# MLA queries made with their features on partitions, in a one-core hybrid encoder block

## The chip, the cores and the metric

The kernel runs on one core of a Trainium2 chip. The metric is device time in microseconds (us) of one execution of the whole block; lower is better. Engines are named as in the profile: PE is the matrix engine (PEld its weight loads), DVE the vector engine, ACT the scalar engine, POOL the GpSimd engine, SP the engine whose queue issues most DMAs.

## The reference, cut to what matters

The block normalises x, multiplies by one input matrix, runs a Mamba-2 mixer (SSD) and a multi-head latent attention (MLA) side by side, projects both out, and then runs a memory cross-attention and a convolutional feed-forward. All is f32, with 512 tokens and width 1024. The change concerns the queries of MLA alone:

```python
q_lat, kv_lat, k_rope = jnp.split(u, [MLA_Q_RANK, MLA_Q_RANK + MLA_KV_RANK], axis=-1)   # 384, 256, 32
q = (rmsnorm(q_lat, q_norm_w) @ w_q_up).reshape(b, s, MLA_HEADS, MLA_NOPE + MLA_ROPE)   # 16 heads of 64 + 32
q_nope, q_rope = jnp.split(q, [MLA_NOPE], axis=-1)
q_rope = apply_rope(q_rope, cos, sin)        # halves t1, t2 of 16: t1*cos - t2*sin, t1*sin + t2*cos
sc = einsum(q_nope, k_nope) + einsum(q_rope, k_rope)
p = softmax(where(mask, sc * (MLA_NOPE + MLA_ROPE) ** -0.5, min))
o = einsum(p, v)
```

## The kernel before, in words

Every f32 product is made of three matmuls (`mm3`, lines 103 to 105): each operand is split into a high part in the matrix engine's f32 format and the rest (`split`, lines 94 and 95: a copy on ACT, then a subtraction on DVE), and the terms high x high, high x low and low x high are added in PSUM. Weights come as pages: `wload` (line 148) has SP load a raw page into one of three `wr` tiles, `wsplit` (lines 156 to 158) splits it into one of four `wh`/`wl` pairs, with half of the subtraction on POOL in the later stages. PSUM has three `acc` banks, two `tr`, two `s` and one `pv`.

The normalised latents lie in five tiles `LT` with features on partitions and all 512 tokens along the row; three of them (384 features) feed the queries. They are filled 128 tokens at a time by `lat_q` and `lat_kv` (through `lat_norm`, lines 614 to 623: a square on ACT, a power on POOL at line 142, a scaling on DVE at line 619, transposes on PE at line 119, splits).

Queries are made four heads at a time by `q_up`. For each of four token tiles, nine matmuls of 384 columns take LT as the stationary operand and the weight page as the moving one, so that tokens lie on partitions (lines 718 to 720). ACT copies the bank to `qrow` (721), and four POOL instructions rotate the rotary features (724 to 727). Later `prep` makes each head ready: `k_pair` makes the keys of two heads by six matmuls of 512 columns, then four PE transposes bring the head's 96 query features onto partitions, and a split writes them into `qts[h % 2]`. There are two query tiles and two key tiles, used by even and odd heads in turn.

The attention loop overlaps heads: `scores(i + 1)`, `prep(i + 2)`, `probs_T(i)` and `pv(i)`, with units of other work put in between (`fills`: the output projection's parts `out_part`, the memory keys and values). `q_up(0)` is named by the operation `U` near the end of the list of the last SSD group; the other three calls stand in the attention loop after heads 1, 5 and 9.

The program order is only a priority. A list scheduler with a timeline model places each engine's instructions when it thinks them ready, and the order it finds is fixed at build time; each engine, and each DMA queue, then runs its list in order and waits at whatever is not ready. Parts of the output projection store and reload their sums through DRAM on the SP queue (`x_d` stores at line 658, loads at line 652), the same queue that issues all weight loads.

Of the kernel before, what the change touches and what calls it, by code (L numbers as in the profile page):

```python
# [7 lines left out]
F32 = mybir.dt.float32  # L8
# [54 lines left out]
def tile_block(ctx, tc, x, mem, positions, norm_mix_w, w_in, ssd_conv_w, ssd_conv_b, ssd_dt_bias,  # L63
# [166 lines left out]
    dec = base.tile([P, 3, NT, SSD_H], F32, name="dec")  # L230
    cenT = base.tile([P, NT, SSD_H], F32, name="cenT")
    acT = dram.tile([NT, SSD_H, P], F32, name="acT")
    memT_d = dram.tile([P, 2, KD, NMEM], F32, name="memT_d")
# [179 lines left out]
    nc.vector.tensor_copy(cosb[:, :, H2:], cosb[:, :, 0:H2])  # L413
    nc.vector.tensor_scalar(sinb[:, :, 0:H2], sinb[:, :, H2:], -1.0, None, ALU.mult)


# [262 lines left out]

    qrow = [k4([P, 2, 4, QH], "qrow") for _ in range(2)]  # L680
    kts, qts = [], []
# [18 lines left out]
    st = {}  # L700
    rts = [k1([P, 4, ROPE], "rt") for _ in range(2)]
    wkh, wkl = (page(n).rearrange("p i (n c) -> p i n c", n=2) for n in ("wkh", "wkl"))
# [6 lines left out]

    def q_up(q4):  # L710
        wq = mla_w_q_up[0][:, q4 * 4 * QH:(q4 + 1) * 4 * QH].rearrange("(k p) c -> p k c", p=P)
        pa = wpage(wq[:, 0:2], 2, 4 * QH)
        pb = wpage(wq[:, 2:3], 1, 4 * QH)
        st["q"] = []
        for t in range(NT):
            acc = acc_bank()[:, 0:4 * QH]
            for k in range(3):
                hi, lo = (pa[0][:, k], pa[1][:, k]) if k < 2 else (pb[0][:, 0], pb[1][:, 0])
                mm3(acc, (LT[k][:, 0, tsl(t)], LT[k][:, 1, tsl(t)]), (hi, lo), k == 0, k == 2)
            r = qrow[t // 2][:, t % 2]  # L720
            nc.scalar.copy(r.rearrange("p h c -> p (h c)"), acc)
            tm = rts[t % 2]
            bc = lambda a: a.unsqueeze(1).broadcast_to([P, 4, a.shape[1]])
            nc.gpsimd.tensor_tensor(tm[:, :, 0:H2], r[:, :, NOPE + H2:], bc(sinb[:, t, 0:H2]), ALU.mult)
            nc.gpsimd.tensor_tensor(tm[:, :, H2:], r[:, :, NOPE:NOPE + H2], bc(sinb[:, t, H2:]), ALU.mult)
            nc.gpsimd.tensor_tensor(r[:, :, NOPE:], r[:, :, NOPE:], bc(cosb[:, t]), ALU.mult)
            nc.gpsimd.tensor_tensor(r[:, :, NOPE:], r[:, :, NOPE:], tm, ALU.add)
            st["q"].append(r)

# [30 lines left out]
    def prep(h):  # L760
        if h % 4 == 0:
            kv_page(h // 4)
        if h % 2 == 0:
            k_pair(h % 4 // 2)
        ps = acc_bank()
        for t in range(NT):
            transpose(ps[0:QH, tsl(t)], st["q"][t][:, h % 4])
        split(qts[h % 2][0:QH, 0], qts[h % 2][0:QH, 1], ps[0:QH])

# [65 lines left out]
    def do(op, i):  # L835
        g, c = seq[i]
        if op == "z":
            z_unit(g, zn.pop(0))
        elif op == "l":
            late.pop(0)()  # L840
        elif op == "d":
            ssd_d(*seq[i - 1])
        elif op == "a":
            ssd_a(*seq[i + 1])
        elif op == "b":
            ssd_b(g, c)
        elif op == "i":
            lat_init()
        elif op[0] == "q":
            lat_q(int(op[1]))  # L850
        elif op[0] == "k":
            lat_kv(int(op[1]))
        elif op[0] == "p":
            part(int(op[1]))
        elif op == "s":
            setup_kq1()
        elif op == "U":
            q_up(0)
        elif op == "S":
            setup_kq2()  # L860
# [38 lines left out]
    for i in range(-1, MLA_H):  # L899
# [12 lines left out]
        if i >= 0:  # L912
            pv(i)
        if i % 4 == 1 and i + 3 < MLA_H:
            q_up((i + 3) // 4)
    for u in fills:
# [280 lines left out]
```

## Time and profile before

| | |
|---|---|
| median of 3 runs | 993.86 us (993.31 to 996.02) |
| the profiled execution, its own time | 995.55 us |
| its span, first to last instruction | 993.8 us |
| busy over the span | PE 98%, DVE 67%, ACT 53%, POOL 28% |
| DMA moved | 114.12 MB, mean 115 GB/s |
| mean granted PE clock | 0.995 of full speed |

The span is what the trace covers; the rest of the profiled execution's time lies around it. Matmuls are pipelined, so the duration of one is longer than the time by which it moves the next one along; the distance between two starts tells what it takes of the engine.

### The profile page before, as it was taken

What the parts mean: (1) busy time and instruction counts of PE and PEld (TensorE: products, weight loads), DVE (VectorE), ACT (ScalarE), POOL (GpSimd) and SP (SyncE); (2) the same over time, 40 slices, a digit from 0 to 9 for tenths busy, and PEclk for the clock granted to TensorE, in tenths of its full rate; (3) what the DMA queues carried; (4) which work ended last, traced back from release to release, by engine and by line L of the source; (5) the groups of instructions that cost most, each with busy time, mean ns of one, the idle gap of its engine ahead of it and who ended that gap; (6) DMA issues with size and microseconds to landing.
All of it is one profiled execution on the core that took longest, in us unless ns stands there. A gap on an engine that the chain in (4) does not pass through costs nothing.

```text
span 993.8 us, 15965 instructions
## 1 busy us (share of the span) xinstructions
PE 972.2 (98%) x5865; PEld 869.5 (87%) x5865; DVE 661.6 (67%) x1226; ACT 524.4 (53%) x1078; POOL 281.2 (28%) x360
## 2 busy tenths in 40 slices
PE   7999999998999999999999999999999999999997
PEld 6889898897899999999988899888888888888886
DVE  5989999868779787763644444676666666622553
ACT  5677776655477777763434433444444444421442
POOL 2016547566653547452343313000000000000000
PEclk9999999999899999999999999999999999999999
DMA  7653432316423336242341212233323322332462
GB/s 232 193 184 101 118 107 76 98 48 186 145 78 102 118 121 216 85 160 83 98 127 64 65 64 86 74 97 107 105 85 96 112 89 85 107 127 88 150 224 90
DMA packets 96453, 114.12 MB, mean 115 GB/s; under 512 B 5799, under 2 KB 82407, under 8 KB 95992
## 3 DMA queue, kind: packets, MB, share of 16 engines
q1 hardware_dynamic: 94680, 106.78, 34.0%
q0 software_dynamic: 1696, 6.33, 2.2%
q8 instruction: 46, 0.75, 0.3%
q14 instruction: 31, 0.25, 0.1%
HBM read 104.67 MB, written 8.42 MB: 114 GB/s over the span
## 4 chain that ended last, share of the span: by engine, by line
PE 83%; DVE 7%; DMA 3%; ACT 3%; POOL 2%; issue 2%; SPq 0%; POOLq 0%; DVEq 0%; ACTq 0%
PE acc L103 22%; PE acc L105 22%; PE acc L104 22%; PE tr L119 3%; PE s L103 2%; PE s L105 2%; PE s L104 2%; PE pv L809 2%; DMA aE<-acT 2%; DVE wl L157 1%; ACT aE L542 1%; DMA x_d<-lat 1%; DMA wr<-in_w_in_dram 1%; PE acc L119 1%; DVE cu L432 1%
## 5 line engine op out<-in xcount | busy, mean ns | idle before, releaser
L103 PE MATMUL acc<-Ah,wh 128*128 128x512 f32 (+1 forms) x560 | 215.7, 385 | 0.2 <-ACT Ah L94 0.2
L104 PE MATMUL acc<-Al,wh 128*128 128x512 f32 (+1 forms) x560 | 215.4, 385 | 0.1
L105 PE MATMUL acc<-Ah,wl 128*128 128x512 f32 (+1 forms) x560 | 215.1, 384 | 0.0
L95 DVE TENSOR_TENSOR wl<-wr,wh 128x1024 fp32r<-128x1024 f32 (+1 forms) x99 | 119.9, 1213 | 102.1 <-ACT wh L94 100.6
L94 ACT CAST wh<-wr 128x1024 fp32r<-128x1024 f32 (+1 forms) x99 | 101.8, 1031 | 135.5 <-PE acc L104 65.3
L158 POOL TENSOR_TENSOR wl<-wr,wh 128x512 fp32r<-128x512 f32 (+2 forms) x64 | 105.1, 1651 | 103.6 <-ACT wh L156 98.2
L142 POOL TENSOR_TENSOR rs<-ms,neg_half 128x1 f32<-128x1 f32 x18 | 10.4, 580 | 404.4 <-DVE ms L140 393.5
L103 PEld LDWEIGHTS acc<-Ah,wh 128*128 128x128 f32 x560 | 105.2, 188 | 20.4 <-ACT Ah L94 0.5
L105 PEld LDWEIGHTS acc<-Ah,wl 128*128 128x128 f32 x560 | 105.3, 188 | 20.1
L104 PEld LDWEIGHTS acc<-Al,wh 128*128 128x128 f32 x560 | 105.3, 188 | 19.9 <-DVE Al L95 0.4
L103 PE MATMUL acc<-wh,Ah 128*128 128x256 f32 (+1 forms) x304 | 90.4, 298 | 1.7 <-ACT Ah L94 1.7
L105 PE MATMUL acc<-wh,Al 128*128 128x256 f32 (+1 forms) x304 | 89.1, 294 | 0.3 <-DVE Al L95 0.3
L104 PE MATMUL acc<-wl,Ah 128*128 128x256 f32 (+1 forms) x304 | 88.9, 294 | 0.0
L156 ACT CAST wh<-wr 128x1024 fp32r<-128x1024 f32 (+2 forms) x64 | 65.5, 1027 | 38.5 <-PE acc L105 12.8
L1091 DVE SCALAR_TENSOR_TENSOR cbuf<-acc,fcw,cbuf 128x511 f32<-128x511 f32 (+1 forms) x88 | 65.6, 747 | 26.6 <-ACT cbuf L1089 25.0
L157 DVE TENSOR_TENSOR wl<-wr,wh 128x512 fp32r<-128x512 f32 (+2 forms) x64 | 55.8, 873 | 40.2 <-ACT wh L156 40.0
L103 PEld LDWEIGHTS acc<-wh,Ah 128*128 128x128 f32 x304 | 58.9, 194 | 2.9 <-ACT Ah L94 2.1
L104 PEld LDWEIGHTS acc<-wl,Ah 128*128 128x128 f32 x304 | 58.9, 194 | 0.5
L105 PEld LDWEIGHTS acc<-wh,Al 128*128 128x128 f32 x304 | 58.6, 193 | 0.9 <-DVE Al L95 0.6
L793 POOL TENSOR_SCALAR p<-p,ri 128x128 f32<-128x128 f32 (+1 forms) x64 | 34.6, 543 | 68.8 <-DVE ri L792 68.0
L1089 ACT ACTIVATE cbuf<-acc,fcb,fcw 128x512 f32<-128x512 f32 x44 | 34.3, 779 | 24.0 <-PE acc L105 24.0
L104 PE MATMUL acc<-wl,act 128*128 128x512 f32 (+1 forms) x112 | 40.5, 363 | 0.0
(370 smaller groups left out, 2450.5 us busy)
## 6 DMA issues: line engine op xcount, KB each, us to landing
wr<-in_w_ffn_up_dram SPq DMA_DIRECT2D x44, 512.0 KB, 3.5
wr<-in_w_ffn_down_dram SPq DMA_DIRECT2D x33, 512.0 KB, 3.6
wr<-in_w_in_dram SPq DMA_DIRECT2D x26, 512.0 KB, 3.8
wr<-in_w_out_dram SPq DMA_DIRECT2D x16, 512.0 KB, 3.7
aE<-acT POOLq DMA_DIRECT2D x16, 256.0 KB, 3.5
wr<-in_w_mem_k_dram SPq DMA_DIRECT2D x8, 512.0 KB, 3.6
wr<-in_w_mem_v_dram SPq DMA_DIRECT2D x8, 512.0 KB, 3.9
wr<-in_w_mem_q_dram SPq DMA_DIRECT2D x8, 512.0 KB, 3.4
```

The source lines that it names most:

```text
L94: first = nc.scalar.copy(hi, src)
L95: nc.vector.tensor_tensor(lo, src, f32(hi), ALU.subtract)
L103: nc.tensor.matmul(acc, lhsT=lh, rhs=rh, start=first, stop=False)
L104: nc.tensor.matmul(acc, lhsT=lh, rhs=rl, start=False, stop=False)
L105: nc.tensor.matmul(acc, lhsT=ll, rhs=rh, start=False, stop=last)
L119: nc.tensor.transpose(dst, src, ident[:n, :n])
L156: nc.scalar.copy(hi, raw)
L157: nc.vector.tensor_tensor(lo[:, 0:a // 2], raw[:, 0:a // 2], f32(hi[:, 0:a // 2]), ALU.subtract)
L158: nc.gpsimd.tensor_tensor(lo[:, a // 2:], raw[:, a // 2:], f32(hi[:, a // 2:]), ALU.subtract)
L793: nc.gpsimd.tensor_scalar(p_, p_, ri, 1.0, ALU.mult, ALU.mult)
L1089: nc.scalar.activation(u, acc, AF.Identity, scale=fcw[:, 2, m:m + 1], bias=fcb[:, m:m + 1])
L1091: nc.vector.scalar_tensor_tensor(u[:, s:], acc[:, :T - s], fcw[:, 2 - s, m:m + 1], u[:, s:], ALU.mult, ALU.add)
```

## The change

Queries are made with features on partitions from the start. `q_rope(g)` makes the rotary features of eight heads at once: the first halves of all eight (8 x 16 = 128 rows) in one bank, the second halves in another, with the weights stationary and LT moving, 512 columns at a time. It rotates them there with cosine and sine tables that have features on partitions (`csT`, made once by eight copies on POOL, eight PE transposes and two ACT copies), and keeps them split in `rq`. `q_pair(pr)` makes the plain features of two heads in one bank, splits them into the two query tiles, and copies the rotary rows of both heads from `rq` by four DMAs. Nothing transposes queries any more. The weights are loaded by pieces: for the rotary features rows of 32 numbers per head, for the plain ones rows of 64. `q_rope(0)` stands where `q_up(0)` stood, `q_rope(1)` after head 4, and `q_pair` in `prep` of every even head. The scratch that POOL-issued DMAs use is set to 8192 bytes per partition.

```diff
+    csT = base.tile([P, 2, T], F32, name="csT")
...
+    csr = k4([P, 2, NT, 8, H2], "csr")
+    for i, tab in enumerate((cosb, sinb)):
+        for t in range(NT):
+            nc.gpsimd.tensor_copy(csr[:, i, t], tab[:, t, H2:].unsqueeze(1).broadcast_to([P, 8, H2]))
+        ps = tr_bank()
+        for t in range(NT):
+            transpose(ps[:, tsl(t)], csr[:, i, t].rearrange("p h c -> p (h c)"))
+        nc.scalar.copy(csT[:, i], ps)
...
-    qrow = [k4([P, 2, 4, QH], "qrow") for _ in range(2)]
+    rq = [k4([P, 2, T], "rq", F32R) for _ in range(2)]
-    rts = [k1([P, 4, ROPE], "rt") for _ in range(2)]
...
-    def q_up(q4):
...
+    def q_rope(g):
+        raw = base.tile([P, 3, 8, ROPE], F32, name="wr", tag="wr", bufs=3)
+        for k in range(3):
+            nc.sync.dma_start(raw[:, k], mla_w_q_up[0][tsl(k), :].rearrange("p (h c) -> p h c", h=MLA_H)[
+                :, 8 * g:8 * g + 8, NOPE:])
+        hi = base.tile([P, 3, 2, 8, H2], F32R, name="wh", tag="wh", bufs=4)
+        lo = base.tile([P, 3, 2, 8, H2], F32R, name="wl", tag="wl", bufs=4)
+        for k in range(3):
+            hv, lv = (a[:, k].rearrange("p s h c -> p h s c") for a in (hi, lo))
+            split(hv, lv, raw[:, k].rearrange("p h (s c) -> p h s c", s=2))
+        acc = []
+        for s in range(2):
+            acc.append(acc_bank())
             for k in range(3):
+                w = [a[:, k, s].rearrange("p h c -> p (h c)") for a in (hi, lo)]
+                mm3(acc[s], w, (LT[k][:, 0], LT[k][:, 1]), k == 0, k == 2)
+        for s in range(2):
+            a, b = f32(rq[s][:, 0]), f32(rq[s][:, 1])
+            nc.vector.tensor_tensor(b, acc[s], csT[:, 0], ALU.mult)
+            nc.vector.tensor_tensor(a, acc[1 - s], csT[:, 1], ALU.mult)
+            nc.gpsimd.tensor_tensor(b, b, a, ALU.add if s else ALU.subtract)
+            nc.scalar.copy(rq[s][:, 0], b)
+            nc.vector.tensor_tensor(rq[s][:, 1], b, f32(rq[s][:, 0]), ALU.subtract)
+
+    def q_pair(pr):
+        raw = base.tile([P, 3, 2, NOPE], F32, name="wr", tag="wr", bufs=3)
+        for k in range(3):
+            nc.sync.dma_start(raw[:, k], mla_w_q_up[0][tsl(k), :].rearrange("p (h c) -> p h c", h=MLA_H)[
+                :, 2 * pr:2 * pr + 2, 0:NOPE])
+        hi = base.tile([P, 3, P], F32R, name="wh", tag="wh", bufs=4)
+        lo = base.tile([P, 3, P], F32R, name="wl", tag="wl", bufs=4)
+        split(hi, lo, raw.rearrange("p k h c -> p k (h c)"))
+        acc = acc_bank()
+        for k in range(3):
+            mm3(acc, (hi[:, k], lo[:, k]), (LT[k][:, 0], LT[k][:, 1]), k == 0, k == 2)
+        for e in range(2):
+            q = qts[e]
+            split(q[0:NOPE, 0], q[0:NOPE, 1], acc[e * NOPE:(e + 1) * NOPE])
+            r = H2 * (2 * pr % 8 + e)
+            for s in range(2):
+                nc.sync.dma_start(f32(q[NOPE + H2 * s:NOPE + H2 * (s + 1)]), f32(rq[s][r:r + H2]))
...
         if h % 2 == 0:
             k_pair(h % 4 // 2)
-        ps = acc_bank()
-        for t in range(NT):
-            transpose(ps[0:QH, tsl(t)], st["q"][t][:, h % 4])
-        split(qts[h % 2][0:QH, 0], qts[h % 2][0:QH, 1], ps[0:QH])
+            q_pair(h // 2)
...
-            q_up(0)
+            q_rope(0)
...
-        if i % 4 == 1 and i + 3 < MLA_H:
-            q_up((i + 3) // 4)
+        if i == 4:
+            q_rope(1)
...
-    nc = _bacc.Bacc("TRN2", target_bir_lowering=False, num_devices=1)
+    nc = _bacc.Bacc("TRN2", target_bir_lowering=False, num_devices=1, dynamic_dma_scratch_size=8192)
```

## Rows read from the trace of the kernel before

**Rows 1.** The page: busy time by engine (PE alone), and the chain that ended last.
```profile
PE 972.2 (98%) x5865; PEld 869.5 (87%) x5865; DVE 661.6 (67%) x1226; ACT 524.4 (53%) x1078; POOL 281.2 (28%) x360
PE 83%; DVE 7%; DMA 3%; ACT 3%; POOL 2%; issue 2%; SPq 0%; POOLq 0%; DVEq 0%; ACTq 0%
```

**Rows 2.** Stretches: length; busy PE, PEld, DVE, ACT, POOL; clock, DMA share, GB/s.
```profile
40.00:100.00 60.00, 60.00 (x357) 52.66 (x356) 54.07 (x102) 43.58 (x87) 20.60 (x26) 1.00 0.46 140
250.00:268.00 18.00, 17.69 (x115) 17.07 (x116) 13.40 (x34) 10.14 (x24) 12.69 (x21) 0.83 0.46 138
268.00:440.00 172.00, 171.88 (x1259) 164.65 (x1259) 136.89 (x331) 126.50 (x323) 87.32 (x134) 1.00 0.39 127
```

**Rows 3.** Timeline of PE around a head's query transposes: start, duration, instruction, count.
```profile
325.94 0.60 PE L119 MATMUL acc<-cst,qrow 128*96 128x128 f32 x4
326.38 0.49 PE L119 MATMUL tr<-cst,p 128*128 128x128 f32 x3
...
330.13 0.34 PE L105 MATMUL acc<-wh,lt 128*128 128x384 f32 x1
...
332.05 0.33 PE L104 MATMUL acc<-wl,lt 128*128 128x384 f32 x1
...
339.68 0.40 PE L103 MATMUL acc<-lt,wkh 128*128 128x512 f32 x1
...
341.07 0.49 PE L119 MATMUL acc<-cst,qrow 128*96 128x128 f32 x3
```

**Rows 4.** Groups by line and shape, PE: busy time and mean ns of one.
```profile
L103 PE MATMUL acc<-wh,lt 128*128 128x384 f32 x48 | 17.2, 358 | 0.4 <-ACT lt L94 0.3
L119 PE MATMUL acc<-cst,qrow 128*96 128x128 f32 x64 | 10.1, 272 | 0.0
```

**Rows 5.** Busy time on tile `qrow` alone: length, PE, PEld, ACT, POOL, clock, DMA.
```profile
236.00:440.00 204.00, 10.09 (x64) 7.32 (x64) 7.67 (x16) 27.57 (x64) 0.98 0.41 131
```

**Rows 6.** Groups by line: two on DVE from 236 to 440 us, one on POOL.
```profile
L95 DVE TENSOR_TENSOR qt<-acc,qt 96x512 fp32r<-96x512 f32 x16 | 10.8, 674 | 0.3 <-ACT qt L94 0.3
L95 DVE TENSOR_TENSOR wl<-wr,wh 128x384 fp32r<-128x384 f32 x3 | 2.8, 935 | 0.4 <-ACT wh L94 0.2
...
L158 POOL TENSOR_TENSOR wl<-wr,wh 128x512 fp32r<-128x512 f32 (+2 forms) x64 | 105.1, 1651 | 103.6 <-ACT wh L156 98.2 <-issue 3.6 <-PE acc L105 1.6
```

**Rows 7.** Timeline of PE before the attention: the first query matmuls and a stall.
```profile
239.64 0.34 PE L103 MATMUL acc<-wh,lt 128*128 128x384 f32 x1
...
247.68 0.34 PE L104 MATMUL acc<-wl,lt 128*128 128x384 f32 x1
250.09 0.90 PE L119 MATMUL tr<-cst,qkl 128*128 128x128 f32 x3 [2.07 <-DVE lt L95]
```

**Rows 8.** Timelines of POOL and of DVE in the same stretch.
```profile
246.65 0.47 POOL L726 TENSOR_TENSOR qrow<-qrow,cosb 128x128 f32<-128x128 f32 x1
...
248.17 1.07 POOL L142 TENSOR_TENSOR rsl<-msl,neg_half 128x1 f32<-128x1 f32 x2
...
248.76 0.62 DVE L619 SCALAR_TENSOR_TENSOR qkl<-lat,rsl,qkl 128x384 f32<-128x384 f32 x1 [2.17 <-POOL rsl L142]
```

**Rows 9.** DMA queue, packets and share of 16 engines; issues by tile, KB each, us to landing.
```profile
q1 hardware_dynamic: 94680, 106.78, 34.0%
...
wr<-in_mla_w_q_up_dram SPq DMA_DIRECT2D x4, 384.0 KB, 4.5
...
x_d<-xs__689 SPq DMA_DIRECT2D x4, 128.0 KB, 1.7
...
x_d<-xs__692 SPq DMA_DIRECT2D x4, 128.0 KB, 3.8
```

**Rows 10.** SP: first query loads, one later load, a wait (us, times, longest).
```profile
206.01 18.01 SPq L148 DMA_DIRECT2D wr<-in_mla_w_q_up_dram  x2
...
349.87 0.38 SPq L148 DMA_DIRECT2D wr<-in_w_mem_k_dram  x1
...
SPq L658 <- DVE xs__689 L657: 10.7, 2, 9.1
```

More of the change, by code (lines that the diff above doesn't have):

```diff
@@ L708, in tile_block @@
     yt = base.tile([P, T], F32, name="yt", tag="L", bufs=5)
-    def q_up(q4):
[L711 to L714, printed above, removed]
-        for t in range(NT):
-            acc = acc_bank()[:, 0:4 * QH]
-            for k in range(3):
[L718 to L728, printed above, removed]
@@ L764, in prep @@
             k_pair(h % 4 // 2)
-        ps = acc_bank()
-        for t in range(NT):
-            transpose(ps[0:QH, tsl(t)], st["q"][t][:, h % 4])
-        split(qts[h % 2][0:QH, 0], qts[h % 2][0:QH, 1], ps[0:QH])
+            q_pair(h // 2)
     POFF = (384, None, 0, 512)
```

## The prediction

> **What bounds the kernel now.** I read the page first: PE is busy for 98% of the span and makes up 83% of the chain that ended last [rows 1]. The busy times by stretch then show where the queries live. From 268 to 440 us, the attention, PE is busy 171.88 of 172.00 us at full clock, with DVE at 80% and ACT at 74% [rows 2]: what PE no longer has to issue there comes off the time, unless something new makes it wait. Just ahead of that, from 250 to 268 us, the granted clock averages 0.83 [rows 2]. As the clock has two levels, 1.2 and 2.4 GHz, PE ran at the lower one for about a third of these 18 us, and (1 - 0.83) x 18 = 3.1 us were lost. The timeline shows what came before: from 239.64 to 247.68 us PE ran 26 of the first query matmuls among other work, then it stood idle for 2.07 us [rows 7]. The other timelines say why. DVE waited 2.17 us for the power on POOL that the last latent tile needs, and POOL had run rotations of the first queries just before it [rows 8].
>
> The price of a matmul is not its duration. A transpose lasts 272 ns [rows 4], but four of them move PE's next instruction by 326.38 - 325.94 = 0.44 us, so one costs 0.11. In the same way a 384-column matmul costs (332.05 - 330.13) / 11 = 0.1745 us and a 512-column one (341.07 - 339.68) / 6 = 0.232 us [rows 3].
>
> **The change, part by part.** *Transposes.* The 64 query transposes go [rows 4]: 64 x 0.11 = 7.0 us of PE. The tables need eight new ones early on: +0.9 us, since PE has no idle time from 40 to 100 us [rows 2].
>
> *Query matmuls.* Before there are 4 x 4 x 9 = 144 of 384 columns (one of their three lines shows 48, [rows 4]), after it 2 x 18 + 8 x 9 = 108 of 512 columns: 144 x 0.1745 = 25.1 us against 108 x 0.232 = 25.0 us. They move the same number of columns; -0.1 us.
>
> *ACT, DVE, POOL.* The 16 copies to `qrow` (7.7 us of ACT) and 64 rotations (27.6 us of POOL) go [rows 5]. ACT gets six 512-column copies instead; by the copies just named, of 384 columns at 0.48 us, that is about 4 us. DVE gets eight multiplications and four subtractions of 512 columns, by the query split at 0.674 us [rows 6] about 8 us, and the subtractions for the weight splits that POOL shared, eight times 0.935 us at most [rows 6]. Both lie in stretches where DVE has a fifth free; I take zero, and up to 2 us if they delay a bank. POOL gets four 512-column additions at 1.65 us [rows 6] and eight small copies. The eight copies have POOL's 39 idle us of 40 to 100 to lie in, while DVE, 90% busy there [rows 2], gets nothing. That the scratch for POOL's DMAs is set anew has no row; between no cost and one landing of 3.8 us [rows 9] I take none, as POOL issues nothing new.
>
> *Weight loads on SP.* Eight loads become 6 + 24 smaller ones, and 32 row copies are new: 54 more issues, at 0.38 us [rows 10] 20 us of a queue that otherwise mostly waits for buffers. A rotary group has 384 x 8 = 3072 rows of 128 bytes. The mean packet of this queue took 0.34 x 16 x 993.8 us / 94680 = 57 ns of one DMA engine [rows 9], whatever its size. So a group takes 3072 x 57 / 16 = 10.9 us and a pair's 768 rows 2.7 us; the row that is nearest, 4.5 us for 384 KB in longer rows [rows 9], is the lower end. The first query loads were out by 224.0 us [rows 10], 15.6 us ahead of their first matmul at 239.64 [rows 7], so even 10.9 us stay hidden. I take zero; the cover ends at 15.6 us.
>
> *Row copies.* The copies for the odd head of a pair wait for the scores of the head two before, and the queue behind them waits too: projection stores and reloads, and weight loads. A pair needs four issues (1.5 us) and a landing between 1.7 and 3.8 us [rows 9], 3.2 to 5.3 us. PE meanwhile has `k_pair` and `q_pair` (15 x 0.232 = 3.5 us), four transposes (0.44 us), `pv` and the fills. The copies may also stand behind a store that itself waits, 9.1 us at the longest [rows 10]. So a pair costs between 0 and 9.1 + 5.3 - 3.9 = 10.5 us. I take zero, because the keys' tiles were already rewritten under the same kind of wait and PE idled 0.12 us in the whole stretch [rows 2].
>
> *The first query pass.* `q_up` could start as soon as one token tile of latents was there; `q_rope` needs all four. The 26 matmuls before the stall (26 x 0.1745 = 4.5 us) must come after it. In their place the scheduler can pull projection parts forward, and POOL's power is no longer behind rotations. Between +4.5 us and more, and -2.1 (the stall) - 3.1 (the clock), I take zero.
>
> *Sum:* -7.0 + 0.9 - 0.1 = -6.2 us. The profiled execution took 995.55 us, 1.75 around its span and 1.7 above the median of 993.86; taken off the median that is 987.7, so **988 us**. The measurement can tell about 0.3%, 3 us, from no change.
>
> A rule of the skill speaks against this change. The Trainium skill, "DMA: Bandwidth & Descriptors" (Specifications and Rules for kernel authors), says that pieces below 512 bytes are read, modified and written, and that small transfers should be put together; by it the 128-byte rows would cost more than the mean packet, up to twice if each is moved twice; no row here shows the price of so short a row. That makes the fourth rival below, whose time is worked out from the rows alone.
>
> **The rivals.** *B, the stall goes with the rotations.* With POOL free of them the last latent tile comes earlier, and both the idle 2.1 us and the clock's 3.1 us vanish: 993.9 - 6.2 - 5.2 = 982.5 us. For it speaks POOL's order in the stretch, against it the loss of 26 matmuls as filling.
>
> *C, the first pass leaves a hole.* Nothing takes the place of the 26 matmuls: -6.2 + 4.5 = -1.7, and with another stretch at 1.2 GHz of the size seen up to +1.4; 993 us. For it: projection parts lean on loads and stores of the same SP queue. Against it: PE ran such parts right after the stall, from pages loaded before it.
>
> *D, the rotary rows come late.* Even and odd heads' query tiles are both rewritten by DMA between the scores of one head and the next. If PE waits at the first scores of each pair, the change loses from 6.2 / 8 = 0.8 us a pair. With one landing of 1.7 us uncovered per pair it is 993.9 - 6.2 + 8 x 1.7 = 1001 us. For it: the queue is strictly in order and full of stores that wait for DVE [rows 10]. Against it: the scheduler lets PE pull other ready matmuls forward, and the stretch had 0.12 us idle.
>
> *E, the short rows come late.* At twice the mean packet time a rotary group takes 21.9 us, 6.3 more than the lead: 994 us. For it there is only the rows' length; against it, the lead and DMA engines that are 39% busy [rows 2].
>
> **How the numbers follow.** The forecast has 0.46, B 0.15, C 0.19, D 0.16, E 0.04. The forecast's own span is 985 to 991. The range takes in B's upper part, C and E, and D where it costs little more than it gives: 982 to 997, which leaves out some 0.13 of D and 0.05 of B. Below 990.9 lie the forecast, B and the edge of C: faster 0.62. C's rest and E give within 0.3%: 0.21. D makes slower: 0.17.
>
> **What would show it.** Right: no `qrow` transposes, 108 query matmuls spaced 0.232 us, PE busy without waits from the first pass to the end of attention, and all of the gain found between 240 and 440 us. B: no idle and full clock around 250 us. C: a longer wait of PE for the latents' splits there, with a lower clock behind it. D: PE waiting for DMAs into the query tiles at the first scores of even heads. E: ACT's split of the rotary weights waiting for its load. The forecast is wrong if PE's idle time between 200 and 440 us grows by more than 3 us, or if the time changes outside that stretch by more than the 0.9 us of the new transposes.

## The result and the profile after

The changed kernel takes 1009.35 us (1008.58 to 1009.43, four runs) against 993.89 us (993.31 to 996.02) for the one before: a ratio of 1.015, 95% interval 1.0132 to 1.0167. It is slower by 15.5 us where 988.0 was forecast, and lies outside the range of 982 to 997.

The page after, with its span, packets, busy PE and chain, the lines that answer to [rows 1]:

```profile
span 1007.6 us, 15840 instructions
PE 971.9 (96%) x5773; PEld 861.8 (86%) x5773; DVE 677.1 (67%) x1244; ACT 523.0 (52%) x1074; POOL 255.0 (25%) x304
DMA packets 108581, 116.22 MB, mean 115 GB/s; under 512 B 18951, under 2 KB 94023, under 8 KB 108120
PE 75%; DVE 11%; issue 5%; ACT 3%; DMA 3%; POOL 1%; SPq 0%; POOLq 0%; DVEq 0%; ACTq 0%
```

PE's share of the span falls from 98% to 96% and its part of the chain from 83% to 75%. Over the whole span it now idles 1007.6 - 971.9 = 35.7 us. To see where, the busy times by stretch (length; PE, PEld, DVE, ACT, POOL; clock, DMA share, GB/s), the last one 172 us from the first scores on, as in [rows 2]:

```profile
40.00:100.00 60.00, 53.78 (x296) 45.93 (x295) 45.54 (x73) 38.94 (x74) 12.50 (x20) 0.94 0.42 133
250.00:268.00 18.00, 13.46 (x78) 11.42 (x77) 14.40 (x41) 8.13 (x28) 10.45 (x15) 0.81 0.40 118
281.00:453.00 172.00, 168.41 (x1173) 155.52 (x1174) 141.03 (x340) 123.28 (x316) 67.30 (x86) 1.00 0.48 144
```

Against [rows 2], PE idles 6.22 us from 40 to 100 us, and its granted clock there falls from 1.00 to a mean of 0.94, so up to (1 - 0.94) x 60 = 3.6 us more are lost at the lower level; the change adds nothing there but two tables. From 250 to 268 us the clock is about what it was, 0.81 beside 0.83. The attention, where PE idled 0.12 us before, now has 3.6 us of idle time. PE's longest waits say what it waited for (total, times, longest, in us):

```profile
PE tr L119 <- DVE msl L140: 4.0, 1, 4.0
PE tr L119 <- DVE mT L95: 3.6, 1, 3.6
PE acc L103 <- DVE cu L442: 2.6, 2, 1.7
...
PE s L103 <- ACT p L820: 1.9, 3, 1.1
```

The first is the last latent tile at 259 us, the next two are the setup, the last is the softmax of the attention.

**Three stretches.** Two instructions that every version has cut the span: the first product of an SSD chunk (`pv<-xs,M`) and the first matmul on the memory attention's output (`acc<-wh,oM`). PE's timelines, before and then after (start, duration, instruction, count):

```profile
80.73 0.45 PE L581 MATMUL pv<-xs,M 128*128 128x128 f32 x3
...
564.91 0.28 PE L103 MATMUL acc<-wh,oM 128*128 128x256 f32 x1
```

```profile
91.63 0.45 PE L591 MATMUL pv<-xs,M 128*128 128x128 f32 x3
...
578.67 0.28 PE L103 MATMUL acc<-wh,oM 128*128 128x256 f32 x1
```

Setup grew by 91.63 - 80.73 = 10.9 us; the middle, where the queries live, went from 484.2 to 487.0, so +2.9 us; the rest is 421.8 to 421.9 us from there to the end of the feed-forward's last matmuls in every version below, and is left out. In the setup the idle time, the clock's part and the 0.9 us of new transposes add up to about 6.2 + 3.6 + 0.9 = 10.7 of these 10.9 us. The forecast had +0.9 and -7.1. So both terms are about 10 us off, with two different causes.

### The profile page after: what moved, and what is told of

Its sections match the earlier page's. It is cut to its first block, busy times and chain, and to the rows that moved or that the text cites. A ratio compares the mean times of both kernels' runs of the same rounds, so it can differ in the third digit from the quotient of the medians.

```text
span 1007.6 us, 15840 instructions
## 1 busy us (share of the span) xinstructions
PE 971.9 (96%) x5773; PEld 861.8 (86%) x5773; DVE 677.1 (67%) x1244; ACT 523.0 (52%) x1074; POOL 255.0 (25%) x304
## 2 busy tenths in 40 slices
DMA packets 108581, 116.22 MB, mean 115 GB/s; under 512 B 18951, under 2 KB 94023, under 8 KB 108120
## 4 chain that ended last, share of the span: by engine, by line
PE 75%; DVE 11%; issue 5%; ACT 3%; DMA 3%; POOL 1%; SPq 0%; POOLq 0%; DVEq 0%; ACTq 0%
PE acc L103 21%; PE acc L104 21%; PE acc L105 21%; PE tr L119 3%; PE s L103 2%; PE s L105 2%; PE s L104 2%; PE pv L839 2%; DVE cu L442 2%; DVE wl L95 1%; DMA aE<-acT 1%; DVE wl L157 1%; DVE aE L554 1%; DMA wr<-in_w_in_dram 1%; DVE y L596 1%
## 5 line engine op out<-in xcount | busy, mean ns | idle before, releaser
L95 DVE TENSOR_TENSOR wl<-wr,wh 128x1024 fp32r<-128x1024 f32 (+2 forms) x109 | 125.8, 1158 | 107.0 <-ACT wh L94 104.5
L94 ACT CAST wh<-wr 128x1024 fp32r<-128x1024 f32 (+2 forms) x109 | 105.9, 977 | 144.2 <-PE acc L104 68.0
L158 POOL TENSOR_TENSOR wl<-wr,wh 128x512 fp32r<-128x512 f32 (+1 forms) x60 | 97.6, 1634 | 114.5 <-ACT wh L156 106.7
L157 DVE TENSOR_TENSOR wl<-wr,wh 128x512 fp32r<-128x512 f32 (+1 forms) x60 | 55.6, 926 | 41.2 <-ACT wh L156 41.1
L156 ACT CAST wh<-wr 128x1024 fp32r<-128x1024 f32 (+1 forms) x60 | 62.3, 1039 | 39.7 <-PE acc L104 14.6
L823 POOL TENSOR_SCALAR p<-p,ri 128x128 f32<-128x128 f32 (+1 forms) x64 | 35.7, 562 | 80.5 <-DVE ri L822 76.3
```

Of the source, the lines that this page charges most:

```text
L94: first = nc.scalar.copy(hi, src)
L95: nc.vector.tensor_tensor(lo, src, f32(hi), ALU.subtract)
L156: nc.scalar.copy(hi, raw)
L157: nc.vector.tensor_tensor(lo[:, 0:a // 2], raw[:, 0:a // 2], f32(hi[:, 0:a // 2]), ALU.subtract)
L158: nc.gpsimd.tensor_tensor(lo[:, a // 2:], raw[:, a // 2:], f32(hi[:, a // 2:]), ALU.subtract)
L823: nc.gpsimd.tensor_scalar(p_, p_, ri, 1.0, ALU.mult, ALU.mult)
```

## The setup: experiments e1 to e5

The loads for the memory's keys show it first. SP's timeline before, then after:

```profile
21.48 0.42 SPq L123 DMA_DIRECT2D mrow<-in_norm_mem_w_dram  x1
22.01 0.89 SPq L421 DMA_DIRECT2D mr<-in_mem_dram  x2
```

```profile
27.10 10.73 SPq L148 DMA_DIRECT2D wr<-in_w_in_dram  x5
37.92 0.53 SPq L123 DMA_DIRECT2D mrow<-in_norm_mem_w_dram  x1
38.50 0.42 SPq L431 DMA_DIRECT2D mr<-in_mem_dram  x1
...
43.19 0.50 SPq L431 DMA_DIRECT2D mr<-in_mem_dram  x1
```

`mrow` is loaded 16.4 us later. Nothing in the change touches it. But the new tile `csr` is taken by `k4`, the helper that hands out thirteen buffers (slots) of one kind, as `mrow` and `mr` are, and stands just ahead of them in the program. POOL writes it late, as the sines and cosines are ready late:

```profile
34.56 1.00 POOL L420 COPY csr<-sinb 128x128 f32<-128x128 f32 x4 [14.15 <-ACT sinb L412]
37.73 1.04 POOL L420 COPY csr<-cosb 128x128 f32<-128x128 f32 x4 [2.17 <-DVE cosb L414]
```

The theory (S): tiles of one kind get their slots in program order, so an early load has to stand behind a tile that is filled late. This happens in the list that is fixed at build time: in the trace SP doesn't wait at `mrow`, it has five weight loads listed ahead of it. The rival is that the eight transposes and copies cost PE, POOL or ACT that much, or that the scratch for POOL's DMAs does.

**e3 and e4: the tables alone, the scratch alone.** e3 is the kernel before with the tables added but unused, and the scratch:

```diff
+    csT = base.tile([P, 2, T], F32, name="csT")
+    csr = k4([P, 2, NT, 8, H2], "csr")
+    for i, tab in enumerate((cosb, sinb)):
...
-    nc = _bacc.Bacc("TRN2", target_bir_lowering=False, num_devices=1)
+    nc = _bacc.Bacc("TRN2", target_bir_lowering=False, num_devices=1, dynamic_dma_scratch_size=8192)
```

e4 has the last line only.

> The kernel before with the tables built as the change builds them, and used by nothing (queries as before, scratch of 8192 bytes). Theory S: the whole setup loss without any of the query work, 993.9 + 10.9 = 1004.8 us. Theory P: 993.9 + 0.9 = 994.8 us, and the loss of the changed kernel lies with its queries.

> The kernel before with the DMA scratch at 8192 bytes and nothing else. Theory S: 993.9 us, no change. Rival R (the smaller scratch delays the DMAs that POOL issues): slower by 3 us or more, with the difference in the stretch of the SSD groups.

e3 took 1004.68 us, ratio 1.0118 (1.0101 to 1.0135); its setup is 90.5 us, its middle 483.4. e4 took 993.98, ratio 1.0004 (0.9994 to 1.0014), with a setup of 79.3 us; that of the kernel before, 80.7, is on the long side. The tables make the whole setup loss without a single query changed, and the scratch costs nothing.

**e1: `csr` from another kind of slot.**

```diff
-    csr = k4([P, 2, NT, 8, H2], "csr")
+    csr = base.tile([P, 2, NT, 8, H2], F32, name="csr", tag="L", bufs=5)
```

> The changed kernel with the table rows csr taken from the five slots tagged L instead of the thirteen tagged k4; nothing else differs. Theory S (the new k4 tile stands ahead of mrow and mr in the order in which slots are given out, so their loads cannot be issued until csr has its slot, 16 us later than before): the loads of mrow and mr go out near 21 us again, PE has no wait from 40 to 100 us, and about 10 us come back: 999 us. Theory P (the eight transposes, copies and ACT reads themselves hold PE up in the setup): no more than 1 us comes back, 1009 us.

1008.23 us, ratio 1.0159 (1.014 to 1.0178): nothing gained in time. Its setup is 88.0 us, 3.65 less than in the changed kernel, but its middle is 2.2 longer. The load is early again. SP's and PE's timelines of e1, and behind them PE's of the kernel before:

```profile
20.90 0.42 SPq L123 DMA_DIRECT2D mrow<-in_norm_mem_w_dram  x1
21.43 0.89 SPq L431 DMA_DIRECT2D mr<-in_mem_dram  x2
```

```profile
46.87 0.93 PE L119 MATMUL tr<-cst,csr 128*128 128x128 f32 x7
47.87 0.27 PE L119 MATMUL tr<-cst,csr 128*128 128x128 f32 x1
52.01 1.04 PE L119 MATMUL tr<-cst,xn 128*128 128x128 f32 x8
59.06 1.03 PE L119 MATMUL tr<-cst,xn 128*128 128x128 f32 x8
```

```profile
37.41 1.04 PE L119 MATMUL tr<-cst,xn 128*128 128x128 f32 x8
44.44 1.03 PE L119 MATMUL tr<-cst,xn 128*128 128x128 f32 x8
```

Only half of S was undone. The tables' transposes also take both `tr` banks ahead of the memory's transposes (`tr<-cst,xn`) in the program, and these now run some 15 us later, behind the late cosines. It is the same queue in a second place.

**e5: other banks as well.**

```diff
-        ps = tr_bank()
+        ps = s_bank()
```

> The run before this one with csr outside k4 gave its loads back but not its time: there the memory's transposes came late instead, behind the two tr banks of the tables. So theory S is widened: both slot queues count, k4 and the tr banks. Here csr comes from the slots tagged L and the tables' two banks from the s banks; the block stays where the change put it. Wider theory S: as fast as with the block moved behind the memory's norm, 999 to 1000 us. Rival (the place of the tables' instructions in the setup itself costs the time): 1008 us.

**e2: the table block moved behind the memory's store.**

```diff
+    mrow = row_tile(k4([P, D], "mrow"), norm_mem_w)
...
+    nc.sync.dma_start(memT_d, f32(mT))
+
     csr = k4([P, 2, NT, 8, H2], "csr")
     for i, tab in enumerate((cosb, sinb)):
```

> The changed kernel with the block that builds the tables moved behind the norm of the memory, csr still in k4. Theory S: the same 10 us come back, 999 us, since mrow and mr now stand ahead of csr. Theory P: 1009 us, as the same instructions are still issued in the same stretch.

e5: 998.82 us, ratio 1.0055 (1.0038 to 1.0072), setup 79.9 us; e2: 999.83, ratio 1.0068 (1.0047 to 1.009), setup 82.7. SP and PE of e5:

```profile
21.06 0.42 SPq L123 DMA_DIRECT2D mrow<-in_norm_mem_w_dram  x1
```

```profile
36.91 1.04 PE L119 MATMUL tr<-cst,xn 128*128 128x128 f32 x8
43.94 1.03 PE L119 MATMUL tr<-cst,xn 128*128 128x128 f32 x8
59.79 0.61 PE L119 MATMUL s<-cst,csr 128*128 128x128 f32 x4
63.17 0.60 PE L119 MATMUL s<-cst,csr 128*128 128x128 f32 x4
```

The memory's chain is back where it was, and the tables, still eight copies and eight transposes, lie behind it at no cost that can be seen: from 40 to 100 us PE is busy again for all of it. S is settled: the loss comes from two queues in program order, one of slots and one of banks. The banks alone are enough to hold the chain back by most of it (e1, setup 88.0 us beside 79.9); the slots alone were not run. Between the medians of the kernel as changed and of e5 lie 10.5 us.

## The middle: what the queries cost by themselves

With the setup repaired the change still loses: e5 by 5.5 us (3.8 to 7.2, from its ratio). So the time of the 64 transposes that went has not come off the whole. The time PE takes from one start to the next, summed by what it ran, shows where they went. This is worked out from PE's timelines, from the last SSD product to the first memory-output matmul (242.1 to 564.9 us before, 252.7 to 578.7 after); a wait counts with the instruction ahead of it:

```
                                      before          after
query transposes                   66    6.10       0    0.00
query matmuls                     135   28.83     108   25.55
SSD matmuls s<-S,bc                 2    0.53       3    4.72
transposes of latents and y        18    2.53      18    4.54
scores                            176   30.38     176   33.28
transposes of probabilities       164   13.91     164   16.19
probabilities x values            132   20.46     129   21.47
```

The columns are instructions and us; nine query matmuls of the kernel before ran ahead of this stretch, and a few transposes are counted to a neighbour's group. The work went as forecast: 6.1 us of transposes are gone, and the query matmuls cost no more (before, 28.83 us hold the stall of 2.07). What came in their place is waiting: 4.2 us behind `s<-S,bc`, which is one hole, 2.0 us around the transposes next to it, and 6.2 us spread over the softmax loop (2.9 + 2.3 + 1.0; these three groups took 64.75 us before and 70.94 after). The granted clock is no part of it: from the last SSD product to the first scores it averages 0.87 before and 0.88 after, and 1.00 from there on in both.

**The hole** lies ahead of the last latent tile's transposes. PE, DVE and POOL of the changed kernel there:

```profile
254.59 0.28 PE L105 MATMUL s<-S,bc 128*128 128x256 f32 x1
258.92 0.90 PE L119 MATMUL tr<-cst,qkl 128*128 128x128 f32 x3 [4.05 <-DVE msl L140]
```

```profile
255.25 1.81 DVE L95 TENSOR_TENSOR wkl<-wr,wkh 128x512 fp32r<-128x512 f32 x2
256.99 0.20 DVE L140 TENSOR_SCALAR msl<-ssl 128x1 f32<-128x1 f32 x2
...
258.26 0.60 DVE L629 SCALAR_TENSOR_TENSOR qkl<-lat,rsl,qkl 128x384 f32<-128x384 f32 x1
```

```profile
256.48 1.17 POOL L601 TENSOR_TENSOR y<-y,gw 128x256 f32<-128x256 f32 x1
257.61 1.06 POOL L142 TENSOR_TENSOR rsl<-msl,neg_half 128x1 f32<-128x1 f32 x2
```

The tile's mean waits behind two splits of key weights on DVE (1.81 us), its power on POOL behind a gate of SSD (1.17 us), then DVE scales; PE waits 4.05 us in one piece. The tile is no later than before: counted from the first SSD product its transposes start at 167.3 us, where they started at 169.4. But the gap ahead of them then held query matmuls and only 2.07 us of waiting [rows 7]. `q_rope` can't start before all four tiles are there, and no other work fills the gap. This is the forecast's rival C. The wait is 4.05 to 4.24 us also in e5, e10, e11, e12, e17 and e18.

## The middle: experiments

Each of these starts from e2 or e5, so the setup is out of the way, or from the kernel before. They are compared by the ratio and by the length of the middle in the profiled execution (before 484.2, e2 485.7, e5 488.8 us; e4, whose instructions are those of the kernel before, has 484.1). The loop is the sum of the table's last three groups: scores, transposes of the probabilities, probabilities x values (before 64.75, e4 64.72, e2 71.2, e5 71.9 us).

**e7: are the row copies late?** The 32 copies of rotary rows are left out, the rows are set to zero once (so the scores lack their rotary part).

```diff
-            for s in range(2):
-                nc.sync.dma_start(f32(q[NOPE + H2 * s:NOPE + H2 * (s + 1)]), f32(rq[s][r:r + H2]))
```

> Tables behind the memory's norm, and the 32 copies of rotary rows into the query tiles are left out (the rows are zeroed once, so the scores lack their rotary part). Theory D: PE's 5.6 us of gaps in the attention go, about 994 us. Theory V: no more than 1 us, about 999 us.

1002.28 us, ratio 1.0088 (1.0073 to 1.0103), middle 490.4, loop 71.1, as in e2: nothing gained. The copies and the short rows of weights were early enough, as the page of the changed kernel has it (size, median us to landing):

```profile
qt<-rq SPq DMA_DIRECT2D x32, 64.0 KB, 2.4
wr<-in_mla_w_q_up_dram SPq DMA_DIRECT2D x24, 64.0 KB, 2.1
wr<-in_mla_w_q_up_dram SPq DMA_DIRECT2D x6, 128.0 KB, 3.0
```

One wait of PE on a copy, 1.0 us, is seen in e5, at the first scores. So D, with a wait for each pair, falls.

**e8: the first pass by halves.** `q_rope` takes 256 tokens at a time, so that its first half needs two latent tiles only.

```diff
-        acc = []
-        for s in range(2):
-            acc.append(acc_bank())
-            for k in range(3):
...
-                mm3(acc[s], w, (LT[k][:, 0], LT[k][:, 1]), k == 0, k == 2)
+        acc = [acc_bank(), acc_bank()]
+        for n in (slice(0, 256), slice(256, 512)):
+            for s in range(2):
...
+                    mm3(acc[s][:, n], w, (LT[k][:, 0, n], LT[k][:, 1, n]), k == 0, k == 2)
```

> Tables behind the memory's norm, and the rotary pass runs by halves of 256 tokens, so that its first half can start when two of the four latent tiles are there. Theory C (the pass that needs all four tiles leaves a hole of about 4 us ahead of the attention): 18 matmuls of 256 columns move ahead of the wait, and 2 us and perhaps some of the lower clock come back, 996 to 998 us. Rival (the hole is POOL's and DVE's chain to the last tile and nothing can fill it, or the two banks held longer stop the parts): 1000 us or more.

1001.27 us, ratio 1.0082 (1.0067 to 1.0097), middle 487.8, loop 72.1. The wait ahead of the last tile fell from 3.60 us (e2) to 2.87, and nothing of it reached the time.

**e11: other filling ahead of the pass.** In the last SSD group two projection parts (`p2`) stand before `U`.

```diff
-PLAN = ('z z z z d a l l b', 'l l d a i q0 k0 p1 q1 b p1 q2 k1 p1 q3 k2', 'p1 d a k3 p1 b p1', 'p1 d U p2 b p3 s S')
+PLAN = ('z z z z d a l l b', 'l l d a i q0 k0 p1 q1 b p1 q2 k1 p1 q3 k2', 'p1 d a k3 p1 b p1', 'p1 d p2 U b p3 s S')
```

> Kernel: the changed one with both repairs of the tables, and in the last SSD group's order two projection parts stand ahead of the rotary query pass instead of behind it. Theory C (the first pass leaves a hole: 26 query matmuls that could run tile by tile filled PE's wait for the last latent tiles, and nothing takes their place): parts of 1.44 us that are ready earlier fill it, and the 4.1 us wait falls by 1.4 to 2.9 us: 996 to 997.5. If the parts are not ready there, or DVE's order sets the wait: 998 to 999.5.

1001.51 us, ratio 1.0078 (1.0058 to 1.0098), middle 490.4; the wait is 4.24 us and a new one of 2.08 us behind POOL's `y` (L601) follows it. The parts ran before the gap, not in it.

**e6, e17, e9: is it DVE?** DVE has the new splits and is 82% busy in the attention (141.03 of 172), 80% before. e6 gives POOL all subtractions of query weights and rotary rows; e17 only those in the loop; e9 does the opposite in the kernel before, where `q_up`'s weight splits, shared with POOL, become DVE's.

```diff
-        split(hi, lo, raw.rearrange("p k h c -> p k (h c)"))
+        rv = raw.rearrange("p k h c -> p k (h c)")
+        nc.scalar.copy(hi, rv)
+        nc.gpsimd.tensor_tensor(lo, rv, f32(hi), ALU.subtract)
```

> Tables behind the memory's norm, and POOL instead of DVE does the subtractions of the query weights' splits and of the rotated rows. Theory V (in the attention DVE, 92% busy where PE now waits, has become the bound): PE's gaps there, 5.6 us, mostly go; about 995 us. Theory D (the DMAs that copy the rotary rows hold the scores up): no change, 999.8 us.

> Kernel: the changed one with both repairs of the tables (998.8 us), and inside the attention loop only (pairs 1 to 7 and the second rotary group) the subtractions of the query weights and of the rotary rows are POOL's instead of DVE's; the first pass is left alone. Theory V (in the loop DVE stands in the way: its in-order queue holds the new query work, some 9 us, ahead of the reductions and splits that the softmax waits for): the attention falls from 298.4 to 294 to 296, the time to 994.5 to 997. Theory L alone (what PE no longer issues turns into waits whatever engine has the rest): 298 and 998 to 999.5.

> Kernel: the one before, with the splits of the query weight pages wholly on DVE (their second halves were POOL's): some 0.9 us more of DVE for each page and none for POOL. Theory V: the loop has so little room on DVE that the attention grows by 1 to 3 us: 995 to 997. Otherwise 993.5 to 994.5.

e6 1003.41 us, ratio 1.0108 (1.0077 to 1.0139); e17 1002.25, ratio 1.008 (1.0062 to 1.0099), middle 491.1, 2.3 more than e5; e9 994.47, ratio 1.0005 (0.9996 to 1.0015), its attention 296.2 us long as before (296.1). Less work on DVE didn't help and more of it didn't hurt. e6 and e17 are not clean, though: POOL takes 1.01 us for a page's subtraction and 1.30 for a row's (e17), where DVE takes 0.67 and 0.69 (e5), so the chains get longer as DVE gets freer. No run shows DVE's load as the cause; that it plays no part in the changed kernel isn't shown either.

**e10, e12, e13, e15: is it the place of the filling?** The three later `q_up` calls, 36 matmuls or 6.3 us each, could be spread over heads 1 to 9, while `q_rope` and `q_pair` are needed at once; and only one filling unit stands in each of heads 0 to 3. e10 gives heads 1 to 12 two units instead of heads 4 to 15, e12 does that and e11, e13 does it to the kernel before, and e15 takes heads 1 to 3 and 7 to 15 and also loads the first key page ahead of the latents' norms.

```diff
-        return int(i < 0 or qi == 1 or (qi == 0 and i > 3))
+        return int(i < 0 or qi == 1 or (qi == 0 and 0 < i < 13))
```

> Kernel: the changed one with the two repairs of the tables (other slots and other banks, 998.8 us), and in the attention loop the second filling unit of a head comes in heads 1 to 12 instead of heads 4 to 15; their number stays 32. Theory F (the three q_up calls of before, 6.3 us each, were filling that PE could take at any time in heads 1 to 9, and the new query work is needed at once; so PE idles where only one filling unit a head is left, 300 to 380 us): the idle 6 us there go, unless they come back in heads 13 to 15, so 993 to 995 us, attention (first scores to the memory queries) 298.4 -> 293. Theory V (DVE or ACT is the bound of a head, or the row copies are late): 998 to 999, attention 298.

> Both edits. If theories F and C hold: 991 to 994 us, level with the kernel before or faster. If neither: 998 to 999.

> Kernel: the one before, with the second filling unit of a head in heads 1 to 12 instead of 4 to 15. Theory F: here the three q_up calls still fill heads 1 to 9, so earlier units bring nothing there and are missing in heads 13 to 15, where PE waited 2.3 us in e10: 994 to 997. If the place of the units decides nothing in either kernel: 993.5 to 994.5.

> Kernel: the changed one with both repairs of the tables (998.8 us); the second filling unit in heads 1 to 3 and 7 to 15 (not 4 to 6); the first page of key weights is loaded and split before the latents' norms instead of among them. Theory F: the waits of 300 to 345 us shrink as in e10 and no unit is missing at the end; with the first hole shorter by up to 1.8 us (the two splits of DVE that stood ahead of the last latent's mean): 993 to 996. If each order only moves the waits: 997.5 to 1001.

e10: 1001.8 us, ratio 1.0078 (1.0055 to 1.01). In the first 80 us from its first scores PE is busy 19.99, 20.00, 19.49 and 20.00 of each 20 us, where e5 has 19.73, 18.71, 18.69 and 20.00: the early waits did shrink. But it waits 2.56 us at 370 us, for a split on DVE, and 2.04 at 462, at the loop's end, where the units are missing. e12: 1007.09, ratio 1.0135 (1.0117 to 1.0153), the worst. e13: 1003.23, ratio 1.0085 (1.006 to 1.0109), also with a wait of 2.05 us at the loop's end. e15: 998.91, ratio 1.0044 (1.0029 to 1.0059), with the one long hole in three pieces of 1.0, 1.46 and 2.0 us. That is level with e5 (1.0055) and still behind the kernel before. Each order moved the waits; none took them away. e13 says something more: with every instruction of the kernel before, in another order, the loop takes 70.7 us instead of 64.75 and the whole is slower by 8.5 us (6.0 to 10.8). An order alone can cost as much as the new queries do.

**e14: what are the transposes worth?** The kernel before, with the 64 query transposes left out and nothing put in their place. The query tiles are split straight from raw query rows, so the scores are other numbers.

```diff
-        ps = acc_bank()
-        for t in range(NT):
-            transpose(ps[0:QH, tsl(t)], st["q"][t][:, h % 4])
-        split(qts[h % 2][0:QH, 0], qts[h % 2][0:QH, 1], ps[0:QH])
+        src = qrow[0].rearrange("p a h c -> p (a h c)")[0:QH, 0:T]
+        split(qts[h % 2][0:QH, 0], qts[h % 2][0:QH, 1], src)
```

> Kernel: the one before, with the 64 query transposes left out and nothing put in their place: the query tiles are filled by the same split from the raw query rows, so the scores are other numbers (part left out: the turning of the queries). It prices the one thing that the change takes away, alone. Theory P (PE is the bound of the attention, and its time there goes down by what PE no longer issues): 60 x 0.1 = 6 us less between first scores and memory queries, 296.1 -> 290, and 987.5 to 988.5 us in all. Theory L (PE keeps pace only because it has as much work as the softmax of a head takes to go through ACT, DVE and POOL; less work of it turns into waiting): 292 to 296, 990 to 993.5 us.

993.21 us, ratio 0.9984 (0.9975 to 0.9994): **1.6 us (0.6 to 2.5) instead of 6 to 7.** Its middle is 562.80 - 80.08 = 482.7, 1.5 us shorter. Even with nothing to pay for, leaving out the transposes brings a quarter of what they take of PE. The distances of starts, summed as in the table, say where the rest went: 6.1 us of transposes are gone, 3.3 come back in the loop (68.0 beside 64.75), and another 1.4 lie ahead of it, in the stretch of the SSD products (162.8 us beside 161.4), which the edit doesn't touch and where the granted clock averaged 0.98 beside 1.00 before. So in the loop itself about 3 of the 6.1 us were won in this execution. Its waits of PE from 270 to 440 us, where the same view of the kernel before lists none:

```profile
PE s L103 <- ACT p L788: 1.3, 5, 0.3
PE s L103 <- DVE p L783: 0.5, 1, 0.5
PE pv L807 <- DVE PT L95: 0.5, 1, 0.5
PE pv L807 <- ACT PT L94: 0.4, 1, 0.4
```

The scores wait for the exponentials that free their bank, `pv` for the split probabilities. The changed kernel, from 281 to 420 us, waits for the same things in its first and third row (the second is a wait at the first scores):

```profile
PE s L103 <- ACT p L820: 1.9, 3, 1.1
PE s L811 <- DVE xo L667: 1.0, 1, 1.0
PE pv L839 <- ACT PT L94: 0.9, 2, 0.5
```

**e18 and e19: work added.** Four units of 12 matmuls that nothing needs, 5.8 us of PE, one in each of heads 0 to 3, in e5 and in the kernel before.

```diff
+    def extra():
+        acc = acc_bank()[:, 0:256]
+        for k in range(4):
+            mm3(acc, (LT[0][:, 0, tsl(k)], LT[0][:, 1, tsl(k)]), (LT[1][:, 0, 0:256], LT[1][:, 1, 0:256]), k == 0, k == 3)
...
+            if qi == 0 and 0 <= i < 4:
+                extra()
```

> Kernel: the changed one with both repairs of the tables (998.8 us), with work added that nothing needs: one unit of 12 matmuls of 256 columns (1.44 us of PE, no other engine) in each of heads 0 to 3, 5.8 us in all. Theory F/L (PE has nothing to do there that is ready, because the query work comes just when it is needed): most of it lies in the idle time, the attention grows by 1 to 3 us, 999.5 to 1002. If the loop is bound by PE's work after all: by 5 to 6 us, 1004 to 1005.

> Kernel: the one before with the same four added units, where PE idles less than 0.2 us in heads 0 to 3: both theories want the attention to grow by 5 to 6 us, 999 to 1000. Only if it grows by much less here as well does PE's busy time hide slack that the trace does not show as idle.

e18: 1006.91 us, ratio 1.0131 (1.0115 to 1.0148), middle 494.9, 6.1 more than e5. e19: 1001.83, ratio 1.0075 (1.006 to 1.009), middle 490.0, 5.9 more. Over the middle, added work costs its full price in both, though the changed kernel waits in just those heads. Over the attention alone, from the first scores on, which the expectations were about, e18 grew by 4.6 us (298.4 to 303.0) and e19 by 7.2 (296.1 to 303.3), and the stretch ahead changed by +1.5 and -1.3. Neither expectation was met: e18 lies between its two theories there and above both in time, e19 above. What the pair shows is that the changed kernel's waits, a few tenths of a microsecond to one each, are no room that other matmuls can use to more than about 1 us.

**What stays open.** That the loop's pace is not set by PE alone is shown by e14: PE waits there for exponentials and split probabilities as soon as it has less to do. Which step of the way from the scores through exponentials, POOL's scaling, transposes and splits is the tightest isn't shown. Of the 6.2 us that the changed kernel's loop gave back, e14 accounts for 3.3; no run finds the cause of the rest. The row copies are not it (e7). An order that fitted the old work and does not fit the new remains a rival, and e13 shows that an order alone can cost that much. It also bears on every small difference here: each edit gives the whole SSD and attention another order of instructions, and the stretch from the first to the last SSD product, which neither e6 nor e10 touches, ran from 159.1 us (e6) to 164.3 (e10), 161.4 before. Of a microsecond or two in one variant that share can't be told from its edit; e6, e7, e10 to e13 and e17 to e19 all came out above every time that was expected of them. And no run closed the hole by itself, so its price below is read from the traces.

## Why the prediction was wrong

**The tables, +0.9 us: the step that failed most.** The prediction counted eight transposes on PE and laid the copies into POOL's idle time. Both are true of the engines: e5 has the same instructions and a setup of 79.9 us. What it left out is what the tables hold: a `k4` slot and both `tr` banks, taken ahead of `mrow`, `mr` and the memory's transposes and used only when the cosines are there. Measured: +10.9 us in the traces, +11.7 us (10.0 to 13.4) by e3; the setup of the kernel before in its trace, 80.7 us, was longer than in five other kernels that have the same one (79.3 to 80.1). No rival had it. The prediction named its own test rightly: "if the time changes outside that stretch by more than the 0.9 us".

**The transposes, -7.0 us.** The price of one, 0.11 us, was a little high: 64 took 6.10 us in the middle. The step from there, "what PE no longer has to issue there comes off the time, unless something new makes it wait", is what failed. It took PE's 171.88 busy us of 172.00 [rows 2] as proof that nothing else bounds. With nothing new at all, e14 gave 1.6 us, and 3.3 of the 6.1 came back in its loop; in the changed kernel 6.2 came back. An engine at 100% says that it is a bound, not how far behind the next one is. The Trainium skill, "Perfetto Trace Analysis" (Identifying the Most-Contended Engine), says that the busy share of PE's matmuls is not a good measure of how close a kernel is to roofline, the most that the engine could do. No run here measures that distance; e14 shows something else about the same share: at 99.9% it did not tell what taking work out would bring.

**The query matmuls, -0.1 us.** Right: 108 were seen in the table above, and they took no more than those before (25.55 us beside 28.83 - 2.07 = 26.76 in that stretch).

**The first pass, zero.** The bounds were right and the choice was not. C said that 26 matmuls (4.5 us) lose their place; they did, and by the table the hole costs 4.2 + 2.0 - 2.1 (the stall that went) = +4.1 us, close to C's price. B was half right. The last tile did come 2.1 us sooner, counted from the first SSD product, but PE's wait for it grew from 2.07 to 4.05 us instead of going, as DVE's splits and SSD's gate stand ahead of the power now. (Some 0.4 of B's 5.2 us were counted twice: over the idle stretch itself the clock already averaged 0.81.) The middle then adds up: -6.1 for the transposes, -1.2 for the query matmuls, +4.1 for the hole and +6.2 for the loop are +3.0 us, beside +2.9 in the trace and +3 for the changed kernel against e3 (ratios 1.015 and 1.0118). For e5, whose order is another again, it is +5.5 (3.8 to 7.2).

**Row copies and weight loads, zero.** Right (e7, and the landings above). The size was off: a rotary group was put at 10.9 us, but its three loads of 128 KB landed 3.0 us after issue each (the median). For the bytes the short rows are dearer, 128 KB in 3.0 us where 384 KB took 4.5 [rows 9]. The Trainium skill, "DMA: Bandwidth & Descriptors" (Specifications), says that transfers under 512 bytes fall short of the line rate, as they are read, modified and written; the landings point the same way. Here the lead hid it, though packets under 512 bytes rose from 5799 to 18951: one split of a pair's weights on ACT waited 3.15 us for its load, at 285 us, but no wait of PE is put down to such a load. The first rotary group's were issued by 219 us and its first product ran at 260.18, so the lead was longer than the 15.6 us counted. D and E fell.

**DVE, ACT and POOL, zero to 2; scratch, zero.** e4 bears out the scratch. For DVE no run shows a cost, but only e9, in the kernel before, is a clean test.

## What to carry to other kernels

A new tile costs more than its instructions: ask which slots and banks it takes, who stands behind it in that queue, and when it is filled. If it is filled late, give it other slots or put it later in the program. And before a saving on the busiest engine is counted in full, take the work out and time that alone; here 1.6 of 6.1 us came off.

## What the runs showed that was not expected

Undoing one of two queues can bring nothing (e1, ratio 1.0159 beside 1.015), undoing both brought 10.5 us. In the same loop, PE work taken out returned 1.6 of 6.1 us (e14), while 5.8 us put in cost 5.9 (e19). And the kernel before, with its filling in another order and nothing else changed, lost 8.5 us (e13), no less than the new queries cost once the setup was repaired. Of the versions with the new queries none beats the kernel before; the best two are e15 (998.91 us) and e5 (998.82 us).
